# Two feed-forward networks by seven half-size block products, and another place for the down factors

## The chip, the cores and the metric

The program runs on one core of a Trainium2 chip. The metric is the device time of that core in microseconds (us), taken as the median of three runs: 2683.75 us for the kernel before (2678.98 to 2688.9). The core has one matrix engine (PE), a vector engine (DVE), an activation engine (ACT), a general engine (POOL) and an engine that here only issues DMAs (SP). Each of them works through its own list of instructions in order.

## The reference

A transformer block over 1024 tokens of width 1024, in fp32, with two gated feed-forward networks (FFNs, hidden width 2816) around a mixing stage:

```
h = x
h = h + 0.5 * swiglu(rms_norm(h, ffn1_norm), ffn1_w_gate, ffn1_w_up, ffn1_w_down)
u = rms_norm(h, mix_norm);  z = u @ w_in
... sparse attention (index scores, top 256 keys, rope) and chunkwise retention on parts of z ...
h = h + merged @ w_out
h = h + 0.5 * swiglu(rms_norm(h, ffn2_norm), ffn2_w_gate, ffn2_w_up, ffn2_w_down)
gate = sigmoid(rms_norm(h, ple_norm) @ w_ple_gate)
h = h + gate * (p @ w_ple_proj)
return rms_norm(h, final_norm)

swiglu(x, w_gate, w_up, w_down) = (silu(x @ w_gate) * (x @ w_up)) @ w_down
```

## The kernel before

Each fp32 product is three matmuls (`split3`): both operands are split into a high and a low part, and high x high, high x low and low x high are summed in PSUM. The split of a weight is an ACT copy (L138, tile `wh`) and a DVE difference (L140, `wl`), that of an activation the same on `uh` and `ul` (L404, L405). Matmuls have 512 columns. `Weights` (`W`) is the planner of the weights: DMAs bring raw blocks of 512 KB into a few `wraw` buffers, a split fills a slot, and a slot comes free with the last product that reads it (`W.release`); the next load, and on from it the next split, is then emitted. The order on PE is that of the code, and on the other engines a scheduler sets it. All DMAs shown here go through SP's one list: an instruction there that waits for its buffer or for its data holds up everything behind it.

**FFN1** (`ffn`, L487) is done straight: for each of 22 tiles of 128 hidden channels 48 gate and 48 up matmuls (`pg`, `pu`), and for each two tiles 96 down matmuls (`pd`), all from one `prod` at L398: 3168 in all. The hidden values stay in SBUF. The residual `hres` is loaded from `x` at the start and updated from each `pd` by DVE (L524). A string `START` sets the order of the start: turns of the tokens (PE transposes L482 into `ntr`, split into `uh` and `ul`) between products of the small embedding `p` (`ptr`, `prod`).

**FFN2** (`Seven`, L541) does the three products by the scheme of Strassen and Winograd: 2 x 2 blocks, seven block products instead of eight, sums and differences of blocks beforehand. For each of 11 pairs j of hidden tiles `blocks` runs seven terms of 12 matmuls for gate and seven for up (`term`, L620; banks `pa` and `pc`; `ev` is a copy out of PSUM, L631). The weight sums for it are four POOL operations for each matrix (L178, L179, L186, L187), the token sums `d` four POOL operations for each couple of token blocks i and i+4 (L593 to L597, in `turn_second`), turned on PE at L580. The hidden sums (POOL, L676 to L679) go to DRAM as seven stores `hf` (L682). `down_factors` (L687) makes the sums of the down weights: one load `wd` of 1 MB (L691), four POOL operations (L693 to L696), four stores `wf` (L698), with one buffer (`bufs=1`). `down` (L700) then reads `hf` and `wf` (or plain weights) back as weights, in seven runs of 132 matmuls (`pda`, `pdc`, L710), 924 in all, and DVE adds them to the residual (L719), which 16 DMAs bring back after the products (L1578).

Of the kernel before, what the change touches and what calls it, by code (L numbers as in the profile page):

```python
# [10 lines left out]
F32 = mybir.dt.float32  # L11
# [36 lines left out]
START = ("R0 R2 P00 P10 T0 P20 P30 P01 T1 P11 R4 T2 P21 R6 P31 T3",  # L48
         "P40 P50 T4 P60 P70 T5 P41 P51 T6 P61 P71 T7")
# [41 lines left out]
class Weights:  # L91
# [3 lines left out]
    def __init__(self, nc):  # L95
        self.nc = nc
        self.raw_free, self.free, self.half_open = [], [], None
        self.loads, self.fills, self.pair, self.rows = [], [], {}, {}
        self.loaded = self.filled = 0
        self.limit = 0  # L100

    def add(self, pool, raws=0, pairs=0):
        self.raw_free += [pool.tile([P, 1024], F32, name=f"wraw{i}") for i in range(raws)]
        new = [Slot(pool.tile([P, 1024], F32R, name=f"wh{i}"), pool.tile([P, 1024], F32R, name=f"wl{i}"))
               for i in range(pairs)]
        self.free += new
        return new
# [24 lines left out]
    def used(self, n):  # L132
        self.loads[n][0] -= 1
        if self.loads[n][0] == 0:
            self.raw_free.append(self.loads[n][2])
# [136 lines left out]
def hybrid_block_kernel(  # L272
# [25 lines left out]
    def ffn_jobs(name, wg, wu, wd):  # L298
        def dn(f):
            W.plain((name, "d", f), 1, D, False, [(0, D, krows(wd, 0, D, f, f + 1))])  # L300

        for f in range(NF):
            tile_job((name, "g", f), wg, f, side=f == 0)
            tile_job((name, "u", f), wu, f, side=f == 0)
            if f % 2 == 0 and f >= 2:
                dn(f - 2)
                dn(f - 1)
        dn(NF - 2)
        dn(NF - 1)

# [9 lines left out]
    def seven_jobs(name, wg, wu, wd):  # L320
        hsp[name] = [dram.tile([P, 7, 512], F32, name=f"h{name}{j}") for j in range(NJ2)]
        wsp[name] = [dram.tile([P, 4, 512], F32, name=f"w{name}{j}") for j in range(NJ2)]
        for j in range(NJ2):
            for m, w in (("g", wg), ("u", wu)):
                W.matrix((name, m, j), *(krows(w, 2 * P * j, 2 * P * (j + 1), 4 * q, 4 * q + 4) for q in range(2)))
        for a in LEFT:
# [35 lines left out]
    ffn_jobs("f1", ffn1_w_gate[0], ffn1_w_up[0], ffn1_w_down[0])  # L362
# [123 lines left out]

    def ffn(name, hres, hid_pool, first, finished, tail):  # L487


        hid = {}  # L490

        def gate_up(f):
            (gh, gl), (vh, vl) = W[name, "g", f], W[name, "u", f]
            hh = hid_pool.tile([P, S], F32R, name=f"hh{f}", tag="hh", bufs=3)
            hl = hid_pool.tile([P, S], F32R, name=f"hl{f}", tag="hl", bufs=3)
            hid[f] = (hh, hl)
            for i in range(2):
                ts = half(i)
                pg = bank("mm", "pg")
                prod(pg, [t for k in range(KT) for t in split3(gh[:, k], gl[:, k], uh[:, k, ts], ul[:, k, ts])])  # L500
                if f == 0 and i == 0:
                    first[0]()
                pu = bank("mm", "pu")
                prod(pu, [t for k in range(KT) for t in split3(vh[:, k], vl[:, k], uh[:, k, ts], ul[:, k, ts])])
                if f == 0 and i == 0:
                    first[1]()
                a = hid_pool.tile([P, 512], F32, name="sg", tag="sg", bufs=2)
                nc.scalar.activation(a, pg, AF.Silu)
                nc.vector.tensor_tensor(a, a, pu, op=OP.mult)  # L509
                split_out(a, hh[:, ts], hl[:, ts])  # L510
            W.release((name, "g", f))
            W.release((name, "u", f))

        def down(f0, last):
            fs = (f0, f0 + 1)
            for b in range(NB):
                for i in range(2):
                    pd = bank("dn", "pd")
                    terms = []
                    for f in fs:  # L520
                        (hh, hl), (wh, wl) = hid[f], W[name, "d", f]
                        terms += split3(hh[:, tok(b)], hl[:, tok(b)], wh[:, 0, half(i)], wl[:, 0, half(i)])
                    prod(pd, terms)
                    nc.vector.scalar_tensor_tensor(hres[:, b, half(i)], pd, 0.5, hres[:, b, half(i)],  # L524
                                                   op0=OP.mult, op1=OP.add)
                    if b == NB - 1 and i == 1:
                        for f in fs:
                            W.release((name, "d", f))
                    if last:
                        if i == 1:  # L530
                            finished(b)
                        for t in tail.get((b, i), ()):
                            t()

        for f in range(NF):
            gate_up(f)
            if f % 2 == 0 and f >= 2:
                down(f - 2, False)
        down(NF - 2, True)

    class Seven:  # L541
# [5 lines left out]
        def open(self):  # L547
# [5 lines left out]
            self.pool = self.top.enter_context(tc.tile_pool(name=f"n{self.name}", bufs=1, side="right"))  # L553
            self.g = self.pool.tile([P, D], F32, name="gain")
            nc.sync.dma_start(self.g, bass.AP(tensor=self.gain.tensor, offset=self.gain.offset,
                                              ap=[[0, P], [1, D]]))
            self.x = {}
# [18 lines left out]
        def turned(self, src, h, l):  # L576
            self.turns = getattr(self, "turns", 0) + 1
            ps = bank(("tr", "mm")[self.turns % 2], "ntr")
# [4 lines left out]
        def turn_first(self, i):  # L583

            return [lambda q=q: self.turned(self.x[i][:, half(q)], uh[:, 4 * q:4 * q + 4, tok(i)],
                                            ul[:, 4 * q:4 * q + 4, tok(i)]) for q in range(2)]
# [18 lines left out]
        def products(self, between):  # L605
# [18 lines left out]
            def blocks(m, j, use):  # L624
# [18 lines left out]
                if m == "g" and j == 0:  # L643
                    for f in between:
                        f()
# [18 lines left out]
            for j in range(NJ2):  # L664
                h = g[j % 2]
                blocks("g", j, silu(h))
# [4 lines left out]
                self.down_factors(sp, j)  # L671
                blocks("u", j, times(h))
                s1, s2, s4 = (sp.tile([P, 512], F32, name=f"s{i}", tag="s", bufs=4) for i in range(3))
# [7 lines left out]
                for q, n in enumerate(LEFT):  # L681
                    nc.sync.dma_start(hsp[self.name][j][:, q], made[n])  # L682
            left.close()
# [3 lines left out]
        def down_factors(self, pool, j):  # L687

            gp = nc.gpsimd
            t = pool.tile([P, 2, 2, 512], F32, name="wd", tag="wd", bufs=1)  # L690
            nc.sync.dma_start(t.rearrange("p f i c -> p f (i c)"), krows(self.wd, 0, D, 2 * j, 2 * j + 2))  # L691
            b11, b12, b21, b22 = t[:, 0, 0], t[:, 0, 1], t[:, 1, 0], t[:, 1, 1]
# [7 lines left out]
        def down(self, hres, finished, turn):  # L700
            bank_plan(mm=4, dn=4)
            sums = [bank("mm", "pda") for _ in range(4)]
# [32 lines left out]
            bank_plan(mm=4, dn=2, tr=2)  # L735
# [10 lines left out]
            run("A22", sums, False, True, {2 + 2 * b: turn_and_next(b) for b in range(4)})  # L746
# [5 lines left out]
    bank_plan(mm=3, dn=3, tr=2)  # L752
    morex = ExitStack()
    more = W.add(morex.enter_context(tc.tile_pool(name="more", bufs=1)), pairs=W_MORE)
    rotx = ExitStack()
# [8 lines left out]
    x0 = x[0]  # L764
    px = ExitStack()
    pk = px.enter_context(tc.tile_pool(name="emb", bufs=1))
    praw = pk.tile([P, NB, 256], F32, name="praw")
    p0 = p[0, 0].rearrange("(b p) c -> p b c", p=P)
    W.limit = 2
    W.load()  # L770
    nc.sync.dma_start(praw[:, 0:4], p0[:, 0:4])
    nc.sync.dma_start(hres[:, 0], x0[tok(0), :])
    norm = Norm(npool, ffn1_norm[0])
    W.load()
    nc.sync.dma_start(hres[:, 1], x0[tok(1), :])
    nc.sync.dma_start(praw[:, 4:8], p0[:, 4:8])
    for b in range(2, NB):
        nc.sync.dma_start(hres[:, b], x0[tok(b), :])
    nc.sync.dma_start(cs, cst)
    nc.vector.memset(mhalf, -0.5)  # L780
    make_identity(nc, ident)
    W.pump()
    for b in range(2):
        norm.scaled(hres[:, b], b)


    pth = pk.tile([P, 2, S], F32R, name="pth")
    ptl = pk.tile([P, 2, S], F32R, name="ptl")
    ppspill = dram.tile([P, NB, D], F32, name="ppspill")

    def turn_p(b):
        ps = bank("tr", "ptr")
        for j in range(2):
            for i in range(2):
                c = (2 * i + j) * P
                nc.tensor.transpose(ps[:, c:c + P], praw[:, b + j, i * P:(i + 1) * P], ident)
        ts = slice(b * P, (b + 2) * P)
        split_out(ps.rearrange("p (k t) -> p k t", k=2), pth[:, :, ts], ptl[:, :, ts])

    def proj_p(b, i):  # L800
        ps = product(("pp", i), b, 2, (lambda k: pth[:, k, tok(b)], lambda k: ptl[:, k, tok(b)]),
                     tag=("mm", "dn")[i])
        t = pk.tile([P, 512], F32, name="ppt", tag="ppt", bufs=4)
        nc.scalar.activation(t, ps, AF.Copy)
        nc.sync.dma_start(ppspill[:, b, half(i)], t)

    for n, w in enumerate(START):
# [870 lines left out]
```

## Time and profile before

| what | us |
|---|---|
| median of the runs | 2683.75 |
| the profiled execution: time / span | 2683.59 / 2681.8 |
| PE busy in the span | 2565.9 (96%), 11812 matmuls and transposes |
| DVE, ACT, POOL busy | 1448.6, 987.1, 613.4 |
| until FFN1's first product | 50.5 |
| FFN1, products and first part of the next stage's work between them | 752.7 |
| FFN2: products / change of stage and first run of down / rest of down | 476.5 / 36.3 / 183.3 |

The span runs from the first to the last instruction; the execution's own time is 1.8 us longer. Busy PE counts an instruction's whole duration, and matmuls overlap, so that the distance from start to start, not the duration, tells what one costs.

### The profile page before, as it was taken

The numbers are of one execution on the slowest core, as the hardware profiler recorded it, in microseconds if no ns is written. First come the engines' busy times: TensorE is split into PE (matmuls) and PEld (weight loads), VectorE is DVE, ScalarE is ACT, GpSimd is POOL, SyncE is SP. The second block draws the span as 40 slices with busy tenths as digits, with TensorE's granted clock in tenths as the row PEclk, the third lists the DMA queues.
The fourth block names the chain that finished last, engine by engine and source line by source line (L and its number), as shares of the span: only waits on it lengthen the run. The fifth ranks groups of instructions, "written<-read, shape, count | busy, mean of one in ns | idle before, by whom it ended". The sixth has DMA issues, their size and how long they took to land. (4 is left out here: it accounts for less than half of the span.)

```text
span 2681.8 us, 32206 instructions
## 1 busy us (share of the span) xinstructions
PE 2565.9 (96%) x11812; PEld 2088.2 (78%) x11812; DVE 1448.6 (54%) x2631; ACT 987.1 (37%) x1745; POOL 613.4 (23%) x498
## 2 busy tenths in 40 slices
PE   8999999999999998888999999999987999999998
PEld 6888888888888787676888887787766788878887
DVE  5433333333357879999456675534534444445564
ACT  5211111111125667662235663423422333334452
POOL 1000000000001333443444431003566544410000
PEclk9999999999999999999999999999998999999999
DMA  7111111111121221221231227652455433376632
GB/s 240 48 47 48 47 48 48 48 47 48 44 87 40 63 77 46 75 62 55 77 88 43 65 63 206 202 165 99 142 185 194 147 99 94 118 268 210 193 103 94
DMA packets 246301, 273.01 MB, mean 102 GB/s; under 512 B 17408, under 2 KB 169216, under 8 KB 246144
## 3 DMA queue, kind: packets, MB, share of 16 engines
q1 hardware_dynamic: 246144, 270.96, 32.2%
q8 instruction: 93, 1.52, 0.2%
q14 instruction: 64, 0.52, 0.1%
HBM read 201.44 MB, written 69.47 MB: 101 GB/s over the span
## 5 line engine op out<-in xcount | busy, mean ns | idle before, releaser
L138 ACT ACTIVATE wh<-wraw 128x1024 fp32r<-128x1024 f32 (+1 forms) x345 | 334.8, 976 | 843.5 <-PE pd L398 202.7
L140 DVE TENSOR_TENSOR wl<-wraw,wh 128x1024 fp32r<-128x1024 f32 (+1 forms) x299 | 363.0, 1221 | 374.8 <-ACT wh L138 371.8
L442 PE MATMUL prod<-wh,uh 128*128 128x512 f32 (+1 forms) x648 | 266.4, 411 | 1.1 <-ACT wh L138 0.9
L442 PE MATMUL prod<-wh,ul 128*128 128x512 f32 (+1 forms) x648 | 257.7, 398 | 0.0
L442 PE MATMUL prod<-wl,uh 128*128 128x512 f32 (+1 forms) x648 | 257.3, 397 | 0.0
L468 POOL TENSOR_TENSOR nst<-nst,mhalf 128x1 f32<-128x1 f32 x24 | 13.1, 549 | 1016.9 <-DVE nst L467 1016.9
L1059 PE MATMUL pgate<-uh,wh 128*128 128x512 f32 x384 | 158.2, 412 | 21.8 <-ACT gt L1066 20.6
L524 DVE SCALAR_TENSOR_TENSOR hres<-pd,hres 128x512 f32<-128x512 f32 x176 | 120.5, 691 | 96.0 <-PE pd L398 95.5
L509 DVE TENSOR_TENSOR sg<-sg,pu 128x512 f32<-128x512 f32 x44 | 30.2, 687 | 248.1 <-PE pu L398 248.1
L1059 PE MATMUL pgate<-ul,wh 128*128 128x512 f32 x384 | 153.2, 399 | 0.0
L1059 PE MATMUL pgate<-uh,wl 128*128 128x512 f32 x384 | 153.1, 399 | 0.0
L442 PEld LDWEIGHTS prod<-wh,ul 128*128 128x128 f32 x648 | 123.6, 191 | 29.1
L1126 ACT ACTIVATE bias<-bias 128x1024 bf16<-128x1024 bf16 (+3 forms) x132 | 117.1, 888 | 63.7 <-DVE bias L1125 62.4
L442 PEld LDWEIGHTS prod<-wh,uh 128*128 128x128 f32 x648 | 124.3, 192 | 19.9 <-issue 1.3
L398 PE MATMUL pd<-wh,hh 128*128 128x512 f32 x352 | 139.6, 397 | 0.0
L398 PE MATMUL pg<-uh,wh 128*128 128x512 f32 x352 | 139.3, 396 | 0.0
L398 PE MATMUL pg<-ul,wh 128*128 128x512 f32 x352 | 139.2, 396 | 0.0
L398 PE MATMUL pu<-uh,wl 128*128 128x512 f32 x352 | 139.2, 396 | 0.0
L398 PE MATMUL pg<-uh,wl 128*128 128x512 f32 x352 | 139.2, 396 | 0.0
L398 PE MATMUL pu<-uh,wh 128*128 128x512 f32 x352 | 139.2, 396 | 0.0
L398 PE MATMUL pu<-ul,wh 128*128 128x512 f32 x352 | 139.2, 396 | 0.0
L398 PE MATMUL pd<-wh,hl 128*128 128x512 f32 x352 | 139.1, 395 | 0.0
(300 smaller groups left out, 6114.5 us busy)
## 6 DMA issues: line engine op xcount, KB each, us to landing
wraw<-in_ffn_w_gate_dram SPq DMA_DIRECT2D x44, 512.0 KB, 3.9
wraw<-in_ffn_w_up_dram SPq DMA_DIRECT2D x44, 512.0 KB, 4.0
wraw<-hf SPq DMA_DIRECT2D x77, 256.0 KB, 3.0
wraw<-in_w_in_dram SPq DMA_DIRECT2D x32, 512.0 KB, 3.8
gspill<-gt SPq DMA_DIRECT2D x48, 256.0 KB, 2.1
wraw<-in_ffn_w_down_dram SPq DMA_DIRECT2D x22, 512.0 KB, 3.5
wd<-in_ffn_w_down_dram SPq DMA_DIRECT2D x11, 1024.0 KB, 5.0
wf<-wd SPq DMA_DIRECT2D x44, 256.0 KB, 2.3
```

The source lines that it names most:

```text
L138: self.nc.scalar.activation(h, src, AF.Copy)
L140: eng.tensor_tensor(l, src, h.bitcast(F32), op=OP.subtract)
L398: nc.tensor.matmul(ps, a, b, start=i == 0, stop=i == n - 1)
L442: nc.tensor.matmul(box[0][:, :cols], a, w, start=k == 0 and i == 0, stop=k == nk - 1 and i == 2)
L468: nc.gpsimd.tensor_tensor(st[:, 1:2], st[:, 0:1], mhalf, op=OP.pow)
L509: nc.vector.tensor_tensor(a, a, pu, op=OP.mult)
L524: nc.vector.scalar_tensor_tensor(hres[:, b, half(i)], pd, 0.5, hres[:, b, half(i)], op0=OP.mult, op1=OP.add)
L1059: nc.tensor.matmul(box[0], a, m, start=k == 0 and j == 0, stop=k == KT - 1 and j == 2)
L1126: nc.scalar.activation(m, m, AF.Copy, accum_out=cnt[:, j:j + 1])
```

## The change

FFN1 becomes a `Seven` as well, and `ffn` and `START` go. Three things in `Seven` itself change for both FFNs: `down_factors(j)` is called after the hidden sums of j instead of before the up product, its 1 MB load becomes four of 256 KB into four tiles that share eight buffers with the hidden sums; the first two terms of gate and of up at j = 0 run before the last couple of token blocks is turned; and turns use the banks `tr` and `dn`. In FFN1, token blocks are loaded, normed and turned in couples (i, i+4) through four `xt` buffers, the products of `p` stand between their turns, the residual is read again from `x` after the products, and the rope tables (DVE, ACT) move behind that.

```diff
-                if m == "g" and j == 0:
-                    for f in between:
-                        f()
+                yield
...
             for j in range(NJ2):
                 h = g[j % 2]
-                blocks("g", j, silu(h))
+                gate, up = blocks("g", j, silu(h)), None
+                if j == 0:
+                    up = blocks("u", j, times(h))
+                    next(gate)
+                    next(up)
+                    for f in between():
+                        f()
+                for _ in gate:
+                    pass
...
-                self.down_factors(sp, j)
-                blocks("u", j, times(h))
-                s1, s2, s4 = (sp.tile([P, 512], F32, name=f"s{i}", tag="s", bufs=4) for i in range(3))
+                for _ in up or blocks("u", j, times(h)):
+                    pass
+                s1, s2, s4 = (sp.tile([P, 512], F32, name=f"s{i}", tag="s", bufs=8) for i in range(3))
...
                 for q, n in enumerate(LEFT):
                     nc.sync.dma_start(hsp[self.name][j][:, q], made[n])
+                self.down_factors(sp, j)
...
-            t = pool.tile([P, 2, 2, 512], F32, name="wd", tag="wd", bufs=1)
-            nc.sync.dma_start(t.rearrange("p f i c -> p f (i c)"), krows(self.wd, 0, D, 2 * j, 2 * j + 2))
-            b11, b12, b21, b22 = t[:, 0, 0], t[:, 0, 1], t[:, 1, 0], t[:, 1, 1]
+            b11, b12, b21, b22 = t = [pool.tile([P, 512], F32, name=f"wd{i}", tag="s", bufs=8) for i in range(4)]
+            for i in range(4):
+                c0 = 512 * (i % 2)
+                nc.sync.dma_start(t[i], krows(self.wd, c0, c0 + 512, 2 * j + i // 2, 2 * j + i // 2 + 1)[:, 0])
...
-    ffn_jobs("f1", ffn1_w_gate[0], ffn1_w_up[0], ffn1_w_down[0])
+    seven_jobs("f1", ffn1_w_gate[0], ffn1_w_up[0], ffn1_w_down[0])
...
+    turns = []
+    for i in range(4):
+        turn_p(2 * i)
+        if i < 2:
+            load_p(2 * i + 4)
+        for b in (i, i + 4):
+            seven.normed(b)
+        weave([lambda b=b, k=k: proj_p(b, k) for b in (2 * i, 2 * i + 1) for k in range(2)], turns)
+        if 1 <= i <= 2:
+            for b in (i + 1, i + 5):
+                load_x(b)
+        turns = seven.turn_first(i)
+        if i < 3:
+            turns = turns + seven.turn_second(i)
+    for f in turns:
+        f()
+    px.close()
+    seven.products(lambda: seven.turn_second(3))
...
+    for i in range(2):
+        for b in range(NB):
+            nc.sync.dma_start(hres[:, b, half(i)], x0[tok(b), half(i)])
     nc.sync.dma_start(cs, cst)
...
-    ffn("f1", hres, hid_pool, [lambda: None, first_tables], normed(mix_norm[0], hres, hspill), tail)
+    finished = normed(mix_norm[0], hres, hspill)
+    seven.down(hres, finished, turn, {4: lambda: W.drop(raws)})
+    for b in range(2):
+        for j in range(2):
+            sm_product(2 * b + j, "dn")
+        turn(b + 4)()
+        finished(b + 6)
```

Two raw buffers more are open during FFN1, as FFN2 had them. The rest of the diff names banks (`m1`), moves a few turns of the stages behind by a place, and puts two empty pieces ahead of the turns in the last product before FFN2.

SP's list in FFN2's products, kernel before, from the first load of down weights on (`wd` and `wf` are the down factors, `wraw` raw weights, `hf` the hidden sums):

```order
L691 DMA wd<-in_ffn_w_down_dram 128x2x1024
L698 DMA wf_86<-wd 128x512 x3
L166 DMA wraw_66<-in_ffn_w_gate_dram 128x4x256
L698 DMA wf_86<-wd 128x512
L691 DMA wd<-in_ffn_w_down_dram 128x2x1024
L698 DMA wf_87<-wd 128x512
L166 DMA wraw_14075<-in_ffn_w_up_dram 128x4x256
L698 DMA wf_87<-wd 128x512 x2
L682 DMA hf_75<-g_14826 128x512
L698 DMA wf_87<-wd 128x512
L691 DMA wd<-in_ffn_w_down_dram 128x2x1024
```

The same place in the changed kernel, from the end of j = 0 on:

```order
L645 DMA wd_15412<-in_ffn_w_down_dram 128x512
L645 DMA wd_15413<-in_ffn_w_down_dram 128x512
L645 DMA wd_15414<-in_ffn_w_down_dram 128x512
L645 DMA wd_15415<-in_ffn_w_down_dram 128x512
L172 DMA wraw_14367<-in_ffn_w_gate_dram 128x4x256
L651 DMA wf_108<-wd_15412 128x512
L651 DMA wf_108<-wd_15413 128x512
L651 DMA wf_108<-wd_15415 128x512
L651 DMA wf_108<-wd_15414 128x512
L172 DMA wraw_65<-in_ffn_w_gate_dram 128x4x256
L172 DMA wraw_14367<-in_ffn_w_up_dram 128x4x256
```

Before, the third load of down weights stands ahead of the hidden sums of j = 0; now one set of four loads and four stores stands behind the seven `hf` stores of each j, and one gate load between its loads and its stores.

SP's list where FFN1's products end and its down begins, changed kernel (`hres` is the residual, `cs` the constants of the rope tables; FFN1 had no such place before):

```order
L645 DMA wd_3563<-in_ffn_w_down_dram 128x512
L155 DMA wraw_66<-hf_85 128x512
L651 DMA wf_96<-wd_3560 128x512
L155 DMA wraw_135<-hf_83 128x512
L651 DMA wf_96<-wd_3561 128x512
L651 DMA wf_96<-wd_3563 128x512
L651 DMA wf_96<-wd_3562 128x512
L155 DMA wraw_135<-in_ffn_w_down_dram 128x512
L155 DMA wraw_65<-hf_84 128x512
L155 DMA wraw_65<-in_ffn_w_down_dram 128x512
L796 DMA hres<-in_x_dram 128x512 x16
L797 DMA cs<-in_cst_dram 128x616
```

The last set of down factors stands between the first loads of the down stage, and behind these the 16 loads of the residual.

PE at FFN2's first terms, kernel before: the last rows of gate's second term (`pc`), and what follows.

```order
L620 MATMUL pc<-ul,wh_71 128x512
L620 MATMUL pc<-uh,wl_72 128x512
L580 MATMUL ntr<-ident,d_14817 128x128 x4
L580 MATMUL ntr<-ident,d_14816 128x128 x4
L580 MATMUL ntr<-ident,xt 128x128 x8
L580 MATMUL ntr<-ident,d_14818 128x128 x4
L620 MATMUL pa<-th,wh_67 128x512
```

And at FFN1's first terms in the changed kernel, where FFN2's stand alike: the last rows of up's second term.

```order
L565 MATMUL pc<-uh,wh_69 128x512
L565 MATMUL pc<-ul,wh_69 128x512
L565 MATMUL pc<-uh,wl_70 128x512
L524 MATMUL ntr<-ident,d_711 128x128 x4
L524 MATMUL ntr<-ident,d_710 128x128 x4
L524 MATMUL ntr<-ident,xt 128x128 x8
L524 MATMUL ntr<-ident,d_712 128x128 x4
L565 MATMUL pa<-th,wh_73 128x512
```

The turns of the last couple stood behind two terms and now stand behind four.

## Rows read from the trace of the kernel before

**Rows 1.** The page's busy times over the whole span.

```profile
PE 2565.9 (96%) x11812; PEld 2088.2 (78%) x11812; DVE 1448.6 (54%) x2631; ACT 987.1 (37%) x1745; POOL 613.4 (23%) x498
```

**Rows 2.** Stretches: length, then busy (instructions) of PE, PEld, DVE, ACT, POOL; clock; DMA.

```profile
0.00:50.50 50.50, 38.11 (x176) 30.05 (x177) 28.64 (x39) 33.99 (x58) 9.85 (x16) 0.97 0.75 258
50.50:803.20 752.70, 751.80 (x3282) 606.56 (x3281) 284.78 (x390) 136.92 (x185) 3.30 (x6) 1.00 0.18 54
1884.40:2094.10 209.70, 177.21 (x716) 140.08 (x716) 92.72 (x94) 59.35 (x93) 142.17 (x98) 0.93 0.54 184
2094.10:2360.90 266.80, 266.76 (x1152) 216.50 (x1153) 118.52 (x136) 91.69 (x136) 114.40 (x77) 1.00 0.34 108
2360.90:2397.20 36.30, 32.57 (x135) 25.90 (x133) 14.25 (x15) 11.84 (x12) 5.86 (x4) 0.95 0.87 308
```

**Rows 3.** FFN1's matmuls on PE in order of time: start, duration, instruction.

```profile
51.06 0.40 PE L398 MATMUL pg<-uh,wl 128*128 128x512 f32 x1
...
55.96 0.40 PE L398 MATMUL pg<-uh,wl 128*128 128x512 f32 x1
```

**Rows 4.** Chain of waits in FFN2's undisturbed products: start, length, what.

```profile
2105.46 5.60 PE pa L620 x24
...
2124.90 5.60 PE pa L620 x24
```

**Rows 5.** Chain of waits, one whole run of FFN2's down.

```profile
2427.21 29.92 PE pda L710 x132
```

**Rows 6.** What PE waited for, 1884 to 2094 us: us, times, longest.

```profile
PE pa L620 <- ACT ev L631: 22.8, 6, 7.7
...
PE ntr L580 <- POOL d L594: 2.7, 1, 2.7
```

**Rows 7.** What SP waited for, 1884 to 2094 us.

```profile
SPq L698 <- DMA wd<-in_ffn_w_down_dram: 43.0, 11, 4.6
SPq L691 <- DMA wf<-wd: 28.0, 13, 4.3
SPq L698 <- POOL wd L693: 16.3, 11, 1.8
SPq L698 <- POOL wd L695: 15.7, 9, 2.6
```

**Rows 8.** Chain of waits in the same stretch, one set of down factors.

```profile
1900.32 4.78 DMA wd<-in_ffn_w_down_dram
...
1911.57 4.18 DMA wf<-wd
...
1915.84 4.99 DMA wd<-in_ffn_w_down_dram
```

**Rows 9.** POOL in order of time, 1895 to 2100 us.

```profile
1896.21 1.26 POOL L596 TENSOR_TENSOR xt<-xt 128x512 f32<-128x512 f32 x1
...
1943.12 1.75 POOL L676 TENSOR_TENSOR s<-g,g 128x512 f32<-128x512 f32 x1
...
1994.19 1.72 POOL L676 TENSOR_TENSOR s<-g,g 128x512 f32<-128x512 f32 x1
...
2046.86 1.73 POOL L676 TENSOR_TENSOR s<-g,g 128x512 f32<-128x512 f32 x1
```

**Rows 10.** DVE's groups until 50.5 us: busy, mean ns, idle before and its releaser.

```profile
L405 DVE TENSOR_TENSOR ul<-ntr,uh 128x512 fp32r<-128x512 f32 x14 | 9.2, 685 | 7.0 <-ACT uh L404 7.0
```

**Rows 11.** DMA issues: KB each, median us from issue to landing.

```profile
wraw<-hf SPq DMA_DIRECT2D x77, 256.0 KB, 3.0
...
wd<-in_ffn_w_down_dram SPq DMA_DIRECT2D x11, 1024.0 KB, 5.0
wf<-wd SPq DMA_DIRECT2D x44, 256.0 KB, 2.3
```

**Rows 12.** SP in order of time, at the start of FFN2's down.

```profile
2377.60 9.32 SPq L1578 DMA_DIRECT2D hres<-h2spill  x13
```

**Rows 13.** DVE's costliest groups in FFN2's undisturbed products.

```profile
L140 DVE TENSOR_TENSOR wl<-wraw,wh 128x512 fp32r<-128x512 f32 (+1 forms) x68 | 74.8, 1102 | 96.0 <-ACT wh L138 96.0
```

## Predicted time

> **What bounds the kernel now.** I read the page's busy times first: PE is busy 96% of the span, DVE 54%, ACT 37%, POOL 23% [rows 1]. The question is therefore how many matmuls go, what one costs, and where the other 4% stand.
>
> The second view is the windows by stage [rows 2]. FFN1's stretch of 752.7 us has PE at 751.8 busy, POOL at 3.3 and the DMA engines at 18%: nothing else is close to a limit there. FFN2's products fall in two parts. In the later one (266.8 us) PE is full; in the earlier one (209.7 us) PE is busy 177.2 us at a mean granted clock of 0.93, and POOL is at 142.2. The reader is to see that the same work runs at two speeds.
>
> The third view gives prices from start to start. FFN1: 21 matmuls from 51.06 to 55.96 us, so 0.2333 us each [rows 3]. FFN2's products: one block of seven terms, 84 matmuls, from 2105.46 to 2124.90, so 19.44 us and 0.2314 each, or 38.9 us for gate and up of one j [rows 4]. Down: 132 matmuls in 29.92 us, 0.2267 each [rows 5].
>
> The fourth view is waits in the slow part. PE waits 22.8 us there for ACT's copy `ev` out of PSUM [rows 6], which is not slow itself: ACT's list has weight splits ahead of it whose raw weights are late. SP's own list tells why: it stands 43.0 us before a `wf` store until the `wd` load has landed, 28.0 before the next `wd` load until the `wf` stores have landed (one buffer), and 16.3 and 15.7 for two of the POOL steps, 103 us of 209.7 in all [rows 7]. The weight loads queue behind these waits. One set of down factors takes 1900.32 to 1915.84, 15.5 us [rows 8], and the eleven follow one another. The sums of j = 0, 1, 2 start at 1943.1, 1994.2 and 2046.9 [rows 9]: 51.9 us a cycle, against 38.9 undisturbed.
>
> **The change part by part.** The sum is made against the profiled execution, 2683.59 us, a span of 2681.8 and 1.8 beside it; it lies 0.16 below the median of the runs.
>
> *FFN1's matmuls.* 3168 x 0.2333 = 739.1 us go. In come 2 x 11 x 84 = 1848 x 0.2314 = 427.6 and 924 x 0.2267 = 209.5, together 637.1. Difference -102. The rest of the 752.7 us, 13.6 us of turns and small products of the next stage, is still woven in and cancels.
>
> *The start.* First product at 50.5 us before. Now 28 turn groups of four transposes take the place of 16, and 16 token sums on POOL come in. Of the 28, five stand behind the first terms, so seven more are on the way to the first product. From below nothing: PE stood idle 50.5 - 38.1 = 12.4 us of the start [rows 2], which could take them all. It is not likely less, since no work leaves the start. From above, POOL's sums stand wholly in line, 16 x 1.26 = 20.2 us [rows 2, 9]. DVE's part of seven turns is 7 x 0.69 = 4.8 us [rows 10], and the couples' second loads come later than single blocks did, since four buffers have to come free. I take +8, nearest to DVE's price with one load of about 3 us behind it [rows 11]. In FFN2's start the turns move behind four terms: the 2.7 us that PE waited for the token sums [rows 6] are covered by two more terms of 2.8 us [rows 4], so -3 there.
>
> *Turns between and the first weights in FFN1.* Five groups of turns behind the first terms, at DVE's 0.69 some 3.5 us [rows 10], and weights that are split while DVE and ACT still work off turns; POOL makes weight sums in FFN1 only now. FFN2's start lost some 10 us of this kind: 48.5 us over the ideal of 696 x 0.2314 = 161 in the first window, less 3 cycles x 13 = 39 for the down factors [rows 2, 9]. Range 2 to 10; I take +6, the middle, since the rows show both ends for one place only.
>
> *FFN1's end of products.* This place is new. In FFN2 the first 132 down matmuls took 36.3 us instead of 29.9, 6.4 lost [rows 2, 5], as the last `hf` must land and be split. In FFN1 the down factors of j = 10 now stand among these loads, and the 16 residual loads stand ahead of the later ones: FFN2's 13 of them held SP 9.3 us [rows 12]. From 6.4 to 6.4 + 9.3 = 15.7; I take +10, since only loads behind the first two or three raw buffers are held. In FFN2 the same factors come in: +2.5 of the same 9.3.
>
> *FFN2's down factors.* They no longer run back to back. One set a j, with 38.9 us to do it; its loads wait for nothing, since eight buffers hold the three sums and four factors of a j with one to spare. What it costs if it fits: 0, so the 3 x 13 = 39 us go; I take -38. What hides it: after the seven `hf` stores the four loads go out, one gate load between them and the stores, POOL needs 4 x 1.3 to 2.2 us, then the stores. SP is held some 3 + 6 us by it, once in 38.9 us, instead of twice or more per 15.5. POOL per j has four hidden sums, eight weight sums and now four factors, at most 16 x 1.75 = 28 of 38.9 us [rows 9]. If the cover is gone, each set costs what it costs before: 13 us a cycle with 51.9 / 15.5 = 3.3 sets in it, so 3.9 us a set.
>
> Here the Trainium skill speaks against the split of the load. The row: 1024 KB land in 5.0 us, 256 KB in 3.0 or 2.3 [rows 11]. By "SBUF — State Buffer", section "The DMA setup-cost knee", every transfer pays about 2 us that do not scale with its bytes, so a few large ones beat many small ones. Taken one after another, four loads at 3.0 would be 12 us instead of 5, seven us more a set; issued one behind the other without a wait between, they overlap, and the set ends about when it did. The forecast takes the latter.
>
> A second rule bears on POOL beside DVE. The row: a hidden sum takes 1.7 us beside DVE's work and a token sum 1.26 [rows 9]; the weight differences `wl` on DVE are 68 x 1.10 us in 267 us [rows 13], PE staying full [rows 2]. By the same page, section "Who interferes with whom", a DVE instruction with two inputs in SBUF and a POOL instruction that reads SBUF exclude one another. The trace agrees as to size, and already has twelve POOL operations a j at full PE; with four more of 1.75 DVE would lose at most 7 of its 21 idle us a j. It changes no term.
>
> *Off the path.* FFN1's 176 residual additions on DVE become 28 (seven times four), and the rope tables move behind the products, where DVE has less to do than in the start; the residual's second read is counted in the transition. Taken at nothing: in FFN1's old stretch DVE was busy 284.8 of 752.7 us [rows 2], and with the seven-product form at 118.5 of 266.8. If DVE were late with the splits, PE would show waits for `wl`.
>
> **Sum.** FFN1: -102 + 8 + 6 + 10 = -78. FFN2: -38 - 3 + 2.5 = -38.5. Together -116.5; 2683.6 - 116.5 = 2567 us.
>
> **Rivals.** *A set of down factors costs wherever it stands.* For: a held SP list delays whatever load is behind it, and the order puts the next gate load between `wd` loads and `wf` stores, its companion behind the stores. Against: in the slow part several sets fell in one cycle, and a weight load has a lead of several us. At 3.9 us a set, FFN2 keeps its 38 and FFN1 gets 11 x 3.9 = 43: 2567 + 38 + 43 = 2648; if only one FFN's sets cost, 2605 to 2610. So 2605 to 2648.
>
> *Start and transition.* The couples hold POOL and the loads in line: start +20 instead of +8, transitions 15.7 in FFN1 and 9.3 more in FFN2: 12 + 5.7 + 6.8 = 24.5, so 2592. For: 16 dependent token sums on an engine that did 16 small things in that time. Against: most of them belong to couples that are not last.
>
> *Slower: spreading the disturbance.* If not the number of sets in a cycle but one hold of SP is what starves the products, then each of 22 cycles takes 51.9 us instead of 38.9: 22 x 13 = 286 more than forecast for both FFNs, 2853 us, slower than before. It decides from 116.5 / 22 = 5.3 us lost per j on, a cycle over 44.2 us. Against: the last 266.8 us of FFN2's products, with all the loads, stores and sums but the factors, run at full PE [rows 2].
>
> *The scheme does not save.* That FFN1's product count falls by one in eight is in the code; that 1848 + 924 matmuls run at FFN2's price is what FFN2 does. Only a lower clock could take it; the clock in the full stretches is 1.00 [rows 2].
>
> **How the numbers follow.** My forecast 0.70, its own range 2549 (start at 0 and the other losses at their lower ends: -8 - 4 - 3.6 - 2.5 = -18, so 2549) to 2585; start and transition in a large form 0.11 (2585 to 2605); sets that cost 0.14 (2605 to 2648); between this and no change 0.02; slower 0.03. The range 2549 to 2615 leaves out most of the third case, the last two and a little below: about 0.18. 0.5%, 13.4 us, is about what a measurement of this kernel can tell from no change: faster 0.95, same 0.02, slower 0.03.
>
> **What would show it.** Right: FFN1's first product at 55 to 65 us; a cycle of the hidden sums of 38.9 us in both FFNs, with PE full in 2 x 428 us; 132 down matmuls after the products in 36 to 46 us; PE without waits for `ev`; SP's waits for `wd` and `wf` still there but once a j. Wrong: cycles of 42 us or more with waits of PE for `ev`; a clock below 1.00 in the middle of the products; a gap of over 15 us between FFN1's products and its down; a first product after 70 us.

## The result, and the profile after

The changed kernel takes 2650.24 us (median of four runs, 2644.29 to 2651.99) against 2683.61 for the kernel before (its four runs beside these): a ratio of 0.9869, 95% interval 0.9854 to 0.9884. It is faster by 33 us, where 116 had been forecast, and lies outside the stated range. The profiled execution has a span of 2650.2 us.

The windows of the changed kernel by stage; columns as in [rows 2]: length, then busy (instructions) of PE, PEld, DVE, ACT, POOL; clock; DMA share and GB/s.

```profile
0.00:67.60 67.60, 45.31 (x204) 35.21 (x204) 36.31 (x49) 38.18 (x68) 35.54 (x36) 0.90 0.56 191
...
114.30:492.50 378.20, 357.34 (x1514) 286.68 (x1513) 171.77 (x181) 119.07 (x180) 217.79 (x145) 0.99 0.44 144
...
532.20:579.50 47.30, 34.37 (x133) 26.06 (x133) 18.32 (x27) 12.29 (x12) 12.78 (x8) 0.87 0.83 278
```

```profile
1853.80:2321.30 467.50, 440.34 (x1867) 353.92 (x1868) 210.18 (x229) 150.46 (x226) 252.66 (x169) 0.98 0.43 139
2321.30:2365.40 44.10, 33.06 (x133) 26.42 (x133) 13.09 (x14) 11.23 (x11) 11.19 (x8) 0.85 0.91 313
```

The first row is the start until FFN1's first product (before: 50.5). The second is nine whole cycles of FFN1's products: 42.0 us each, where 38.9 is what the matmuls need [rows 4]. The third is the change of stage in FFN1, 132 down matmuls that need 29.9 [rows 5]. The last two are FFN2's products, 467.5 us against 476.5 before, and its change of stage, 44.1 against 36.3. FFN1's products run from 67.6 to 532.2 us, 464.6 in all. So of the 38 us that FFN2 was to get back [rows 2] only 9 have come: the rest is now a loss of about 3 us in a cycle, and FFN1 has it too.

What PE waits for in those nine cycles, then rows of what SP and ACT wait for there (us in total, times, longest):

```profile
PE pa L565 <- ACT ev L576: 20.9, 9, 2.7
```

```profile
SPq L651 <- POOL wd L646: 32.3, 9, 4.2
SPq L651 <- POOL wd L649: 16.5, 9, 1.8
SPq L651 <- POOL wd L647: 11.4, 9, 2.1
SPq L651 <- POOL wd L648: 8.7, 9, 1.0
SPq L172 <- DVE wl L146: 107.1, 18, 7.5
```

```profile
ACT wh L144 <- DMA wraw<-in_ffn_w_gate_dram: 49.7, 7, 7.5
```

PE stops once a cycle, always before the third term, which goes on in a PSUM bank that ACT has to copy out first (`ev`). SP stands 69 us before the four `wf` stores (L651), 7.7 a cycle. It stands longer, 107 us, until a weight buffer is free (L172); that wait is still 86 us in e1 below, where PE is full. ACT's split of a weight waits 49.7 us for a gate load. One cycle shows how the one becomes the other. First SP, then ACT, then PE, each in order of time: start, length, instruction, idle time before it and its releaser.

```profile
293.56 0.38 SPq L172 DMA_DIRECT2D wraw<-in_ffn_w_gate_dram  x1
297.61 6.04 SPq L651 DMA_DIRECT2D wf<-wd  x4
303.74 0.39 SPq L172 DMA_DIRECT2D wraw<-in_ffn_w_gate_dram  x1
```

```profile
300.01 0.61 ACT L602 ACTIVATE g<-ev 128x512 f32<-128x512 f32 x1
308.13 0.63 ACT L144 ACTIVATE wh<-wraw 128x512 fp32r<-128x512 f32 x1 [7.50 <-DMA wraw<-in_ffn_w_gate_dram]
308.67 0.58 ACT L602 ACTIVATE g<-pa 128x512 f32<-128x512 f32 x1
309.15 0.62 ACT L144 ACTIVATE wh<-wraw 128x512 fp32r<-128x512 f32 x1
309.67 0.59 ACT L576 ACTIVATE ev<-pa 128x512 f32<-128x512 f32 x1
```

```profile
310.31 0.50 PE L565 MATMUL pa<-th,wh 128*128 128x512 f32 x1 [2.74 <-ACT ev L576]
```

The second gate load of the next pair goes out at 303.74, when the last store has gone. It lands at about 308; ACT has stood 7.5 us before its split, and behind that split stand three short instructions, the last of them the copy that PE needs. PE does not need the weight yet, since it is still in the up product of the pair before it. It is late only for ACT's list.

### The profile page after: what moved, and what is told of

Its sections match the earlier page's. It is cut to its first block, busy times and chain, and to the rows that moved or that the text cites. A ratio compares the mean times of both kernels' runs of the same rounds, so it can differ in the third digit from the quotient of the medians.

```text
span 2650.2 us, 32857 instructions
## 1 busy us (share of the span) xinstructions
PE 2489.3 (94%) x11464; PEld 2030.7 (77%) x11464; DVE 1514.1 (57%) x2640; ACT 1100.8 (42%) x1900; POOL 899.4 (34%) x688
## 5 line engine op out<-in xcount | busy, mean ns | idle before, releaser
L146 DVE TENSOR_TENSOR wl<-wraw,wh 128x1024 fp32r<-128x1024 f32 (+2 forms) x422 | 521.0, 1241 | 542.9 <-ACT wh L144 528.2
L565 PE MATMUL pa<-th,wh 128*128 128x512 f32 x352 | 142.8, 406 | 43.2 <-ACT ev L576 43.2
L1029 PE MATMUL pgate<-uh,wh 128*128 128x512 f32 x384 | 159.2, 415 | 20.9 <-ACT gt L1036 19.8
L663 PE MATMUL pda<-wh 128*128 128x512 f32 x352 | 140.3, 399 | 21.4 <-ACT wh L144 10.7
L565 PE MATMUL pa<-ul,wh 128*128 128x512 f32 x352 | 141.2, 401 | 4.7 <-DVE ul L402 4.7
L565 PE MATMUL pa<-th,wl 128*128 128x512 f32 x352 | 142.7, 405 | 0.0
L565 PE MATMUL pa<-uh,wh 128*128 128x512 f32 x352 | 140.6, 399 | 1.8 <-ACT uh L401 1.8
L565 PE MATMUL pa<-tl,wh 128*128 128x512 f32 x352 | 142.0, 403 | 0.0
L565 PE MATMUL pa<-uh,wl 128*128 128x512 f32 x352 | 140.8, 400 | 0.0
L565 PE MATMUL pc<-uh,wl 128*128 128x512 f32 x352 | 139.7, 397 | 0.0
L565 PE MATMUL pc<-ul,wh 128*128 128x512 f32 x352 | 139.6, 396 | 0.0
```

The costliest lines, as they stand in the source:

```text
L146: eng.tensor_tensor(l, src, h.bitcast(F32), op=OP.subtract)
L565: nc.tensor.matmul(ps, x_, y_, start=start and k == 0 and i == 0, stop=stop and k == 3 and i == 2, skip_group_check=True)
L663: nc.tensor.matmul(ps[i], x_, y_, start=start and j == 0 and n == 0, stop=stop and j == NJ2 - 1 and n == 2, skip_group_check=True)
L1029: nc.tensor.matmul(box[0], a, m, start=k == 0 and j == 0, stop=k == KT - 1 and j == 2)
```

## The experiments

All times are medians of four runs, and the ratios are to runs of the kernel before on the same chip. Theory A, which the trace above suggests: the stores hold SP, SP the load, the load ACT, ACT the copy. Rivals: POOL's own time (B) and the traffic (C).

**e1: the stores behind the second gate load.** The POOL operations and loads stay; the stores are emitted later and put behind the last matrix load on SP.

```diff
-            for q, d in enumerate((b11, b22, b12, b21)):
-                nc.sync.dma_start(wsp[self.name][j][:, q], d)
+            self.kept = lambda: [nc.sync.dma_start(wsp[self.name][j][:, q], d)
+                                 for q, d in enumerate((b11, b22, b12, b21))]
...
+                if j:
+                    with tc.issue_after(W.last.ins):
+                        self.kept()
```

> In both FFNs the four stores of the down factors (wf) stand one place later on SP's list, behind the second gate load instead of ahead of it; nothing else moves. Theory A (the stores, waiting on SP for POOL, hold the second gate load some 8 us; its split on ACT stands ahead of the copy ev that PE waits for): a cycle of the hidden sums falls from 42.0 to at most 39.5 us in both FFNs, PE's waits for ev nearly go, the time is about 2600 us. Theory B (POOL's own time for the factors delays the weight sums): the cycle stays at 42, the time at 2650. Theory C (the traffic of the factors slows the weight loads): the same, 42 and 2650.

2591.34 us, ratio 0.965 (0.9634 to 0.9667). The sums of FFN1 now follow one another by 38.9 us (the last by 40.1), and PE waits for `ev` nowhere in the stretch. SP in one cycle, and the window of the nine cycles:

```profile
282.04 2.69 SPq L173 DMA_DIRECT2D wraw<-in_ffn_w_gate_dram  x2
286.11 5.72 SPq L656 DMA_DIRECT2D wf<-wd  x4
```

```profile
114.20:464.20 350.00, 350.00 (x1514) 283.98 (x1513) 166.51 (x181) 121.05 (x180) 219.08 (x145) 1.00 0.47 156
```

The same 1514 instructions take 350.0 us instead of 378.2; POOL has as much to do and the DMA engines move as much. ACT's waits for a gate load are gone from the stretch. Only the order of five rows of a cycle on SP's list differs. The time came out 9 us under the forecast of A, as the cycle fell to 38.9 us and not to 39.5. Products take 436.4 and 436.7 us in the two FFNs.

**e2 to e4: three other ways to lift the hold.** e2 issues the stores from POOL (`nc.gpsimd` in place of `nc.sync`), e3 leaves out the four POOL operations, e4 the whole set.

```diff
 e3
-            gp.tensor_tensor(b11, b12, b11, op=OP.subtract)
-            ... the three after it
 e4
-                self.down_factors(sp, j)
...
-                    wap = wsp[name][j][:, t:t + 1]
+                    wap = krows(wd, 512 * (t % 2), 512 * (t % 2) + 512, 2 * j + t // 2, 2 * j + t // 2 + 1)
```

> The four stores of the down factors are issued by POOL behind its own sums instead of by SP. Theory A: no hold on SP, cycle at most 39.5 us, about 2600 us, as long as an issue costs POOL under about 1 us. Theory B: cycle 42 or more, since POOL has more to do, 2650 or more. Theory C: 42, 2650.

> The four POOL operations of each set of down factors are left out (loads and stores stay; the stored factors are plain weights). Theory A: the stores wait only for the loads, SP is held about 5 us less, cycle 39 to 40, about 2605 us. Theory B: the cycle is 38.9 to 39.5, about 2600. Theory C: traffic is as before, cycle 42, 2650.

> The down factors are left out whole: no loads, sums and stores; the down stage reads plain weights in their place, so bytes read in down are the same. All theories: cycle 38.9 us in both FFNs, 28 us less in each. Beyond it the change from products to down, now 47.3 and 44.3 us, loses the last set, which stands between its loads: theory A 36 to 39 us in each. Together about 2575 us; if the changes stay as long, 2594.

2593.42 (0.9657), 2584.34 (0.9625) and 2570.86 us (0.9572). Cycles are 38.9 us in all three, as in e1, but for one of 40.0 us in FFN1 and one of 39.3 in FFN2 of e3, whose time is 21 us under A's forecast. e1 and e2 tell A from B and C, since both leave POOL's sums and the traffic as they were; e3 alone would not have told A from B. In e4, where the last set is missing too, the changes of stage take 33.2 and 33.7 us, against 46.6 in FFN1 and 43.8 in FFN2 in e1. What a set costs in the products is then nothing; what the last one costs in these 132 matmuls is 13 and 10 us. Not all of it is gained: the rest of down, from its first start to its last, takes 186.3 and 184.9 us in e4 against 182.9 in both FFNs in e1, so that 10 and 8 us are left.

**e5 to e7: the change of stage.** In the changed kernel SP shows two holds in FFN1's change of stage, and PE's long stop comes behind the second:

```profile
549.52 3.06 SPq L651 DMA_DIRECT2D wf<-wd  x3
...
555.49 10.41 SPq L796 DMA_DIRECT2D hres<-in_x_dram  x16
566.24 0.33 SPq L797 DMA_DIRECT2D cs<-in_cst_dram  x1
566.92 0.33 SPq L155 DMA_DIRECT2D wraw<-in_ffn_w_down_dram  x1
```

```profile
573.71 0.80 PE L663 MATMUL pda<-wh 128*128 128x512 f32 x1 [9.37 <-ACT wh L144]
```

e5 makes each set half a cycle earlier on top of e1; e6 spreads the residual loads over the first down run on top of e1; e7 does both.

```diff
 e5
+                self.down_factors(sp, j)
                 for _ in up or blocks("u", j, times(h)):
                     pass
+                with tc.issue_after(W.last.ins):
+                    self.kept()
 e6
-            run("A11", sums, True, False)
+            run("A11", sums, True, False, {3 + 2 * n: lambda n=n: residual(n) for n in range(4)})
```

> On top of e1 (late stores) the set of down factors of each j is made half a cycle earlier, after gate instead of after the hidden sums, so that the last set no longer stands among the first loads of the down stage. Theory D (the last set on SP is what makes the change of stage long): the 132 matmuls from products to the second run, 46.5 us in FFN1 and 43.8 in FFN2 in e1, take 33 to 36 in both, as in e4 without sets (33.2 and 33.8); cycles stay at 38.9; about 2570 us. Theory E (the 16 residual loads and the constants ahead of the weight loads are what makes it long): no change in FFN1, 46; a time of 2585 to 2591.

> On top of e1 alone: the residual loads, constants and rope tables are spread behind the fourth, sixth, eighth and tenth weight pair of the first down run; the last set of factors stays where it was. Theory D: FFN1's change of stage still holds the set; it loses at most the 9 us for which PE waited behind the residual loads, 37 to 46 us, FFN2's stays at 41 to 44, where PE's long wait comes before those loads; 2582 to 2591. Theory E: both fall to 33 to 36, about 2570.

> Early sets (e5) and the later residual loads (e6) together. Theory D: as e5, 33 to 36 us in both, about 2570. Theory E: as e6, about 2570. If each holds SP in turn: only here are both at 33 to 36, and e5 and e6 are at 38 to 44.

2571.18 (0.958, interval 0.9562 to 0.9598), 2578.22 (0.9612) and 2574.43 us (0.9595). The window of the change of stage in e5 and in e6, FFN1:

```profile
503.20:536.20 33.00, 31.21 (x134) 24.59 (x132) 14.03 (x19) 9.43 (x9) 6.84 (x4) 1.00 0.90 313
```

```profile
503.30:538.00 34.70, 31.48 (x134) 24.60 (x133) 15.38 (x13) 10.55 (x11) 12.89 (x8) 1.00 0.77 250
```

In FFN1 either is enough: 33 and 34.7 us against 46.6. There the set and the residual loads have to come together to cost 13 us, so that neither D nor E holds alone (D gave e6 at least 37 us, E gave e5 46). In FFN2 only the set counts: 32 us in e5, 44.2 in e6, where PE still stops for 10.7 us ahead of any residual load. That is as D said. e7 gains nothing over e5 (36.6 us in both stages, just above the 33 to 36 forecast). In e5 too part comes back in the rest of down (186.3 and 184.4 us), which in e6 and e7 stays at 182.9: the whole down stages of e5 are 21 us shorter than those of e1, and the time is 20 us shorter.

**e9: the sets as before, in the changed kernel.** One buffer, one load of 1 MB, after gate, so that they follow one another: three things go back together.

> The changed kernel with the down factors as before: one load of 1 MB, one buffer, issued after gate, so that the sets follow one another from j = 0 on; all else as changed. Theory A (each hold of SP costs the products some 3 us, wherever it stands): FFN1's products take 468 to 480 us and FFN2's 470 to 478, against 464.6 and 467.5 paced; the last set leaves the changes of stage, 36 to 40 us against 47.3 and 44.3; the time is 2640 to 2655, no different from the changed kernel: the pacing as made is worth nothing. Theory P (the pacing removed part of the loss, and the changes of stage are long for other reasons): 2665 to 2680.

2663.68 us, ratio 0.9923 (0.9906 to 0.994). FFN1's products take 482.5 us, FFN2's 486.0, and PE waits 65 us for `ev` in the two together (43 in the changed kernel):

```profile
PE pa L565 <- ACT ev L576: 65.3, 13, 7.9
```

In FFN1 the first three cycles take 60.0, 57.8 and 43.2 us, and those from the fifth on 38.9. The changes of stage take 33 us each, without a set in them. Both theories miss: A's upper ends were too low by 2.5 and 8 us in the products and by 9 in the time, and P, whose total was missed by 1.3 us, had the changes of stage long for other reasons, which they are not. The sum is another: the sets as changed (paced, in four loads, half a cycle later) took some 18 us from the products of each FFN and gave back 14 and 11 in the change of stage. Against e1's 436.4 us, eleven sets cost FFN1 46 us in one burst and 28 spread out.

**e8, e10 to e12: the start.** Four tries at the 17 us. e8 (on e7) issues the 16 `ppspill` stores (the projected embedding) from ACT and puts token sums on POOL behind the power (`nst`) in the next couple's norm; e10 (on e5) takes the weight sums of the first gate back until the third couple is normed; e12 is e5 with the ACT stores, e11 is e10 with them.

```diff
 e8, e11, e12
-        nc.sync.dma_start(ppspill[:, b, half(i)], t)
+        nc.scalar.dma_start(ppspill[:, b, half(i)], t)
 e10, e11
-    W.limit = len(W.loads)
+    W.limit = 4
...
+        if i == 2:
+            W.limit = len(W.loads)
+            with tc.issue_after(seven.nst.ins), tc.issue_after(seven.sq.ins):
+                W.pump()
```

> On top of e7, in FFN1's start: the 16 stores of the projected embedding are issued by ACT behind the copy that makes them, not by SP, and on POOL the token sums of a couple stand behind the norm's power of the next couple. Theory F (an in-order list again: SP held before ppspill, POOL's power behind four sums of 1.3 us, twice 3.9 us of DVE): FFN1's first product at 58 to 63 us instead of 67.7, 5 to 9 us less than e7. Theory G (the work of the start is what it is: buffers of couples, 28 turn groups): 66 to 69, as e7.

> On top of e5, in FFN1's start: gate's weight sums and the next weight loads and splits are taken back until the third couple of token blocks is normed (ACT waited 6.4 us for POOL's weight sum at 22 to 28 us, with token work behind it). Theory H (that wait on ACT's list is what makes the start longer): FFN1's first product at 58 to 63 us instead of 67.0, with no new wait for weights behind it, 2560 to 2566. Theory G (couples and their four buffers set the start): 66 to 68, as e5. If weights are then late: the first product is early, but j = 0 ends no earlier than in e5 (113.3 us).

> e10 with the 16 stores of the projected embedding issued by ACT instead of SP. If SP's list held the second loads of token blocks: 2 to 5 us less than e10 until the first product. If the buffers do: the same within 1 us, or up to 3 more, since ACT issues 16 DMAs.

> e5 with those 16 stores issued by ACT alone. Theory H: the wait on ACT stays, first product at 64 to 67 us. If SP's list was the hold: 60 to 63.

FFN1's first product comes at 77.1 us in e8, 67.6 in e10, 65.6 in e11 and 70.1 in e12; in the nine profiles with the start unchanged (the changed kernel, e1 to e7 and e9) it comes at 67.0 to 69.4. Theories F and H, which had 58 to 63 us for e8 and e10, are not borne out: the waits that they named get shorter (DVE's for POOL's power 4.0 us in e8 against 10.4 in e7, ACT's for POOL's weight sum 3.7 in e10 against 6.9 in e5), and the start does not. In e8 and e12 another wait has grown, PE's for ACT's `pt`: 14.7 and 13.9 us, against 3.9 in e7 and 3.7 in e5. The ACT stores make the start 2 us shorter on e10 (the least that was forecast if SP's list is the hold) and 3 longer on e5 (longer than either forecast), hardly more than the 2.4 us by which the nine profiles differ. The times are 2585.14, 2571.12, 2568.10 and 2573.59 us. Two lists show longer waits in the changed kernel's start. ACT's wait for POOL's weight sum is new, and SP's for ACT's copy of the projected embedding has grown; the last row is the same wait in the kernel before:

```profile
ACT wh L144 <- POOL wraw L185: 6.4, 1, 6.4
```

```profile
SPq L760 <- ACT ppt L759: 34.1, 15, 9.8
```

```profile
SPq L805 <- ACT ppt L804: 19.6, 8, 8.5
```

What makes the start 17 us longer stays open. That PE's, ACT's and DVE's work in it grows is in the windows (45.3, 38.2 and 36.3 us against 38.1, 34.0 and 28.6, at a clock of 0.90 against 0.97 [rows 2]); none of the four tries separated this from the order of the couples. The fastest version is e11, 2568.10 us, ratio 0.956 (0.9546 to 0.9575), not told apart from e5 (0.9562 to 0.9598).

## Why the prediction was wrong

*Matmuls.* Right. The products run at 38.9 us a pair as soon as nothing holds them (e1), and the rest of down takes 184 us in FFN1 as 183.6 in FFN2: the term of -102 is there.

*FFN2's down factors, -38, and the same sets at nothing in FFN1.* This is the step that failed. Of the 85 us between the forecast and the profiled execution (2651.99 us) 63 lie in the products: FFN1's took 464.6 us where 433.6 were forecast, FFN2's 467.5 where 435.5 were. Moving the stores alone gives 59 us back (e1). The text said that SP is held some 3 + 6 us by a set, once in 38.9 us, and cost that at nothing. The hold was sized about right, 7.7 us a cycle of waiting; what was not worked out is what stands behind it. The prediction had the chain itself (raw weights late, ACT's list held, `ev` late) from the slow part, and named the gate load behind the stores as its first rival's reason; against it, it counted a lead of several us, without saying up to which instruction. Up to the weight's use on PE there is such a lead. Up to its split on ACT's list, ahead of the copy `ev`, there is none: PE stood 2.3 us for `ev` in each of the nine pairs from the second to the tenth. The prediction's own sign of being wrong, cycles of 42 us or more with waits of PE for `ev`, is what came.

*The rival "a set costs wherever it stands"* (2605 to 2648, chance 0.14) is nearest to the result, which lies 2 us above it, with 3.1 us a set instead of 3.9; its reason, the held SP list ahead of the gate load, is what the runs showed. In its words it fell as well: a set costs nothing in e1, only its place does.

*Four small loads, and POOL beside DVE.* The loads of 256 KB took a median of 4.3 us to land in the changed kernel, four overlapping, against 5.0 for 1 MB [rows 11], and PE is full in e1 with four loads a set and with POOL's work unchanged. So the rule of the Trainium skill ("SBUF — State Buffer", section "The DMA setup-cost knee") that a few large transfers beat many small ones changed nothing in the products, as forecast. Neither did its rule that a DVE instruction with two inputs in SBUF and a POOL instruction that reads SBUF exclude one another (the same page of the Trainium skill, section "Who interferes with whom").

*Change of stage.* FFN1: +10 forecast, 17.4 measured, outside the range of 6.4 to 15.7; FFN2 +2.5 forecast, +7.8 measured. The parts were right, the last set and the residual loads; the sizes were too small. In FFN1 the two cost what they do only together (e5, e6); in FFN2 it is the set alone.

*Start.* +8 forecast, +17.1 measured, within the bounds of 0 to 20.2 and near the end that was thought unlikely. The mechanism is open, as said.

*Slower rival.* That one hold of SP a cycle is enough to starve the products is what the runs showed; it had put 13 us on it, and 3.1 were measured, under its point of decision of 5.3.

With the stores in place and the last set out of the way (e5), the kernel takes 2571 us; 2567 had been forecast. That is partly luck: the start is 9 us longer and the changes of stage 14 us shorter than the sum had them, of which some 5 come back behind them.

## What to carry to other kernels

The lists of SP and ACT were worked off in order here, so the lead of a load is not the time until its data is used: it is the time until the first instruction that waits for it, and what waits behind that instruction decides. Before spreading a burst over a loop, write down for one turn of the loop what stands behind each waiting DMA on the queue, and what stands behind the instruction that waits for that load. When a hold is found, try the order first: here moving four stores by one place on SP's list gave 59 us, more than the whole change, with no work left out.

## What the runs showed of the hardware

The nine stops cost more than their length. In the nine cycles PE stood still 20.9 us, but they lost 28.2: the same 1514 instructions were busy for 357.3 us at a mean granted clock of 0.99 in the changed kernel and for 350.0 at 1.00 in e1. Of the other 7.3 us some 4.7 are clock. After three of the nine stops (2.65, 2.74 and 2.30 us long) the granted clock fell to 0.50, which is 1.2 GHz, soon after PE had started again, and the next eight or nine matmuls followed one another by up to 0.43 us instead of 0.23. The second of them, as a window and as rows:

```profile
311.50:314.50 3.00, 3.00 (x8) 2.31 (x8) 2.50 (x4) 0.00 (x0) 1.35 (x1) 0.50 0.51 133
```

```profile
311.65 0.63 PE L565 MATMUL pa<-th,wl 128*128 128x512 f32 x1
312.08 0.63 PE L565 MATMUL pa<-th,wh 128*128 128x512 f32 x1
```

After the other six, one of them of 2.71 us, the clock stayed at 1.00. The remaining 2.5 us are 0.27 us at each of the nine stops: the last matmul before it is not overlapped by a next one, and the first after it takes 0.34 us to the next start instead of 0.23. In FFN1's change of stage the 132 matmuls were busy 34.4 us at 0.87 and 31.2 at 1.00 in e5.
